# During a scan, the low parts of split weights on VectorE, scaled states and an affine map on ScalarE

## The chip, the cores and the metric

The kernel runs on one core of a Trainium2 chip. The metric is the time of one launch on the device, in microseconds (us), as the median of several runs; the kernel before has 3870.33 us (three runs, 3869.77 to 3872.68). The engines are named as in the profile: PE is TensorE's matmul and PEld its weight load, DVE is VectorE, ACT is ScalarE, POOL is GpSimd, and SP is SyncE, which issues most of the DMAs here. Each engine works off its own queue in order, and waits on semaphores for the others.

## The reference, cut to what matters

One layer of an encoder is applied to two groups of tokens: 512 prompt tokens and 1024 sample tokens, each of width 1024. It is a SwiGLU (inner width 2816), then a mixer, then a second SwiGLU, each with an RMSNorm before and after it, and with shift, scale and gate vectors that come from a conditioning vector.

```python
x = x + 0.5 * mod[:, 2] * rmsnorm(swiglu(h, f1_w1, f1_w3, f1_w2), n1_post)
z = h @ w_in                                  # 1024 -> 512 + 1952
m = concat([pool_mixer(z[..., :512]), rwkv7_mixer(token_shift(z[..., 512:]))])
x = x + mod[:, 5] * rmsnorm(m @ w_out, nm_post)
x = x + 0.5 * mod[:, 8] * rmsnorm(swiglu(h, f2_w1, f2_w3, f2_w2), n2_post)
```

The recurrent half of the mixer (8 heads of 64, two directions) is a scan over the tokens with a state S of 64x64 per head:

```python
def step(S, inp):
    r_t, w_t, k_t, v_t, na_t, b_t = inp
    sa = einsum('bhvk,bhk->bhv', S, na_t)
    S = S * w_t + sa[..., None] * b_t[:, :, None, :] + v_t[..., None] * k_t[:, :, None, :]
    return S, einsum('bhvk,bhk->bhv', S, r_t)
```

with `k_d = k * (1 + (a - 1) * kah)` for each direction. Everything is float32.

## The kernel before, in words

**Dense products.** The tokens are held in three blocks of 512 (sample 0, sample 1, prompt), features on the partitions. A float32 product is made of three fast matmuls: weights and activations are each split into a high part (`whi`, `hh`, `gh`), which is a rounded copy, and a low part (`wlo`, `hl`, `gl`), which is the value less its high part. A tile of weights, 128x512, is loaded by SP (`wraw`), rounded on ACT (`whi`), and subtracted (`wlo`, lines 498 to 505); then `mm3` issues high x high, high x low and low x high, each 128x512, which are called dense matmuls below. A tile is split three tiles before it is used.

**The scan.** It is done in chunks of 64 tokens. A macro step handles a pair of heads, in both directions and for two groups of four chunks (`gi` 0 and 1); there are 12 macro steps. Four kinds of processes carry it:

- `scan_prep` makes the decays and scaled operands of a group (`sg`, `ta`, `cs`, `AR`, `BK`, and `kd` in the tile `in_wa`: the affine map `ta * kah + kam`, line 1220, then times k), and the masked products of the chunk (`MU`).
- `scan_inv` inverts 16 triangular 64x64 matrices of a group at once. DVE transposes their diagonal 32x32 blocks from `MU` into `XN`, 62 dependent small tensor-tensor operations solve them in `XN` (on DVE for gi 0, on POOL for gi 1), DVE transposes back into `MU`, and two bursts of 16 small matmuls into a PSUM tile `sM` finish the off-diagonal blocks. The two inverses of a macro step exclude each other.
- `scan_state`, one per direction, goes through the chunks. Per chunk: matmuls for W into the bank `sb`, a copy on ACT to the upper rows of `XN` (`wsb`, line 1351), the old state times its decay (`s0p`, line 1354), matmuls with the inverse, a copy on ACT to `MU`, matmuls for the output and the new state, and the update of `SBD` on DVE from PSUM and `s0p`.
- `scan_post` normalizes the finished outputs.

While the scan runs, the first SwiGLU of the prompt tokens, the input product of the prompt tokens and the first output products fill TensorE between the scan's small matmuls.

**What sets the order.** The queue order of every engine is written out ahead by a planner in the kernel: an `Estimate` holds for each engine the time when it is free and for each tile when it is ready, from a table of costs (a subtraction of 128x512 counts 597 ns on DVE and 1226 on POOL). `run_until` steps the processes, the scan's before the dense ones where both are ready by that estimate. The engine of a low part is chosen by it: POOL, unless POOL is estimated over 4000 ns late and later than DVE (lines 502 to 504). `pick` chooses likewise between DVE and POOL for some adds of the norms and the posts. Since the helpers record every operation, nearly all instructions have line 161 in the profile; tiles tell them apart.

Of the kernel before, what the change touches and what calls it, by code (L numbers as in the profile page):

```python
# [12 lines left out]
AF = mybir.ActivationFunctionType  # L13
ALU = mybir.AluOpType
# [21 lines left out]
POOL_LATE = 4000  # L36
# [136 lines left out]
def encoder_kernel(ctx, tc, x_prompt, x_sample, c_prompt, c_sample, ada_w, ada_b, n1_pre, n1_post,  # L173
# [5 lines left out]
    V, S, G, T, SY = (Queue(est, *q) for q in (("V", nc.vector), ("S", nc.scalar), ("G", nc.gpsimd), ("T", nc.tensor),  # L179
                                               ("Y", nc.sync)))  # L180
# [33 lines left out]
    def spawn(gen, prio):  # L214
        procs.append(Proc(gen, prio))
# [36 lines left out]
                p_.ready = max(est.last + (AFTER_STATE if p_.prio == 0 else AFTER_OTHER), est.free["T"] + (0.0 if r == WAIT else r))  # L252

    flags = set()

    def until(f):
        while f() > est.free["T"] + 100:
            yield (f(),)
# [18 lines left out]
    def has(*k):  # L277
        return lambda: all(x in flags for x in k)
# [71 lines left out]
    kah = ct([P, 4], name="kah")  # L350
    kam = ct([P, 4], name="kam")
# [130 lines left out]
    class WStream:  # L482
# [12 lines left out]
        def split(self, upto):  # L495
            while self.ns <= min(upto, len(self.items) - 1):
                self.load(self.ns)
                t = self.raw.pop(self.ns)
                wh = mt([P, TB], "whi", 5, F32R)
                wl = mt([P, TB], "wlo", 5, F32R)  # L500
                S.activation(wh, t, AF.Copy)
                now = est.free["T"]
                g_, v_ = max(now, est.free["G"]) + 1200, max(now, est.free["V"]) + 600
                E = G if g_ < now + POOL_LATE or g_ < v_ else V
                E.tensor_tensor(wl, t, wh.bitcast(F32), ALU.subtract)
                self.out[self.ns] = (wh, wl)
                self.ns += 1
# [650 lines left out]
    def scan_prep(sb):  # L1158
        AR, BKt, UV, MU, Pt, PL = sb.AR, sb.BKt, sb.UV, sb.MU, sb.Pt, sb.PL
# [27 lines left out]
        for n, (m, gi) in enumerate(groups):  # L1187
            i_, hf = macros[m]
            g, p = pairs[i_]
# [14 lines left out]
            ta = st_(sb, [P, 2, GL], "ta")  # L1204
            for i, (dst, wt, o) in enumerate(((sg, w2s, 0), (ta, a2s, 8))):
# [5 lines left out]
                for d, pl in enumerate(pls):  # L1211
                    S.activation(dst[:, d, :], pl[:, 0:GL], AF.Tanh,
                                 bias=w0h[:, o + 4 * d + p:o + 4 * d + p + 1], scale=0.5)
# [3 lines left out]
            for d in range(2):  # L1217
                V.tensor_tensor_scan(rd[d](cs[:, d, :]), rst, rd[d](sg[:, d, :]), 0.0, ALU.mult, ALU.add)
            kd = ld["wa"]
            G.tensor_scalar(kd, ta, kah[:, p:p + 1], kam[:, p:p + 1], op0=ALU.mult, op1=ALU.add)  # L1220
            yield WAIT
            pinv = sg
            S.activation(flat(pinv), flat(cs), AF.Exp, scale=DECAY_C)
# [59 lines left out]
    def scan_inv(sb, gi):  # L1283
# [7 lines left out]
        eye = bass.AP(tensor=e_.tensor, offset=e_.offset, ap=[list(e_.ap[0]), [-2, 16], [1, 32]])  # L1291
        E = (V, G)[gi]
        for m in range(len(macros)):
# [37 lines left out]
    def scan_state(sb, d):  # L1331
        AR, BKt, UV, MA, MR, SBD, PL, bank = sb.AR, sb.BKt, sb.UV, sb.MA, sb.MR, sb.SBD, sb.PL, sb.bank[d]
        Wp = bank[0:64, 0:P]
        Up = bank[0:64, P:2 * P]
        for m, (i_, hf) in enumerate(macros):
            g, p = pairs[i_]
            nblk = GT[g] // GL
            nh = nblk // 2
            for c8 in range(8):
                gi, c = c8 // 4, c8 % 4  # L1340
                if c == 0:
                    yield has(("inv", m, gi))
                zero = hf == 0 and c8 == 0
                lastc = hf == nh - 1 and c8 == 7
                us = [gi * 16 + d * 8 + h * 4 + c for h in range(2)]
                if not zero:
                    mm(Wp, AR[:, gi, d, c, 0, :], SBD[:, d, :], stop=False)
                for h in range(2):
                    mm(Wp[:, h * L:(h + 1) * L], MA[64:128, us[h], :], UV[64:128, gi, d, c, h, :], start=zero)
                wsb = sb.iw[:, d * P:(d + 1) * P]  # L1350
                S.activation(wsb, Wp, AF.Copy)
                if not zero and not lastc:
                    s0p = st_(sb, [P, P], f"s0p{d}")
                    G.tensor_scalar(s0p, SBD[:, d, :], PL[:, m % 2, gi, d, c:c + 1], 0.0, op0=ALU.mult, op1=ALU.add)
                yield WAIT
                for h in range(2):
                    mm(Up[:, h * L:(h + 1) * L], MA[0:64, us[h], :], wsb[:, h * L:(h + 1) * L])
                S.activation(UV[0:64, gi, d, c].rearrange("p h f -> p (h f)"), Up, AF.Copy)
                yield WAIT
                if not lastc:  # L1360
                    for h in range(2):
                        hs_ = slice(64 * h, 64 * h + 64)
                        mm(bank[hs_, 0:L], BKt[:, gi, d, c, hs_], UV[:, gi, d, c, h, :])
                yo = 256 + c * L
                if not zero:
                    for h in range(2):
                        hs_ = slice(64 * h, 64 * h + 64)
                        mm(bank[hs_, yo:yo + L], SBD[hs_, d, hs_], AR[hs_, gi, d, c, 1, :], stop=False)
                for h in range(2):
                    mm(bank[64 * h:64 * h + 64, yo:yo + L], UV[:, gi, d, c, h, :], MR[:, us[h], :], start=zero)  # L1370
                if not lastc:
                    for h in range(2):
                        hs_ = slice(64 * h, 64 * h + 64)
                        pl_ = PL[hs_, m % 2, gi, d, c:c + 1]
                        if zero:
                            V.tensor_scalar(SBD[hs_, d, hs_], bank[hs_, 0:L], pl_, None, op0=ALU.mult)
                        else:
                            V.scalar_tensor_tensor(SBD[hs_, d, hs_], bank[hs_, 0:L], pl_, s0p[hs_, hs_],
                                                   ALU.mult, ALU.add)
                if c == 3:  # L1380
                    t = 2 * hf + gi
                    gb = t if d == 0 else nblk - 1 - t
                    if t == 0 and i_ not in sb.yT:
                        if i_ >= 1:
                            yield has(("post", i_ - 1))
                        if i_ not in sb.yT:
                            sb.yT[i_] = st_(sb, [P, GT[g]], "yT")
                    o = sb.yT[i_][:, gb * GL:(gb + 1) * GL]
                    if d == 1:
                        o = rev(o)  # L1390
                    if t >= nh:
                        V.tensor_tensor(o, o, bank[:, 256:512], ALU.add)
                    else:
                        S.activation(o, bank[:, 256:512], AF.Copy)
                    flags.add(("st", m, gi, d))
                yield WAIT
# [182 lines left out]

    with tc.tile_pool(name="late", bufs=1, reuse_waits="tile") as lp:  # L1580
        sb = ScanBufs(lp)

        spawn(scan_state(sb, 0), 0)
        spawn(scan_state(sb, 1), 0)
        spawn(scan_inv(sb, 0), PRIO_INV)
        spawn(scan_inv(sb, 1), PRIO_INV)
        spawn(scan_prep(sb), PRIO_PREP)
        spawn(scan_post(sb), PRIO_POST)

        run_until(has(("m", 1), ("m", 0)))  # L1590

    with tc.tile_pool(name="tail", bufs=1, reuse_waits="tile") as tp:

# [32 lines left out]
```

## Time and profile before

| | |
|---|---|
| median of the runs | 3870.33 us (3869.77 to 3872.68) |
| the profiled execution | 3878.62 us, its span 3876.6 us |
| mean granted TensorE clock | 0.936 of full speed |
| busy in the span: PE, DVE, ACT, POOL | 3649.0, 1977.2, 1364.7, 1704.0 us |
| the scan (first to last of its instructions) | about 1200 to 2810 us of the span |

The profile is of one execution. A row of the groups reads: line, engine, operation, written tile <- read tiles, partitions x elements, count, then the busy time in us and the mean ns of one, then the time that the engine sat idle before such instructions and what ended it. A row of the stretches has the stretch and its length, the busy us of the engines with the number of instructions, the granted clock as a share of full speed, the share of the DMA engines and GB/s. A row of the waits has who waited for whom, us in total, how often, and the longest.

### The profile page before, as it was taken

To read this page: it belongs to the slowest core of one execution; us is meant where nothing else is said; L and a number is where in the kernel's file an instruction comes from. 1 tells how busy PE (TensorE), PEld (TensorE's weight loads), DVE (VectorE), ACT (ScalarE), POOL (GpSimd) and SP (SyncE) were. 2 spreads that over 40 slices of the span, in tenths; PEclk is the share of its full clock that TensorE was granted. 3 is DMA by queue.
4 is the path that set the end of the run, shared out by engine and by line. 5 is a ranking of instruction groups with operands and counts; after the bars stand their busy time and mean duration, and the time that the engine had idled before them with its cause. 6 is when DMAs were issued, how large, how long until landed. Compare 5 with 4: busy or idle time off the path is not lost. (4 is left out here: it accounts for less than half of the span.)

```text
span 3876.6 us, 53921 instructions
## 1 busy us (share of the span) xinstructions
PE 3649.0 (94%) x19579; PEld 2752.9 (71%) x19579; DVE 1977.2 (51%) x3633; ACT 1364.7 (35%) x2592; POOL 1704.0 (44%) x2068
## 2 busy tenths in 40 slices
PE   7999999998999999999889988899999999999998
PEld 4667778876776667666667666566777778877886
DVE  3127352245247557765876676766348632232223
ACT  3324342234444333333334333333234432233222
POOL 2334444442233554355445355445544344444444
PEclk8999999999999989999879787789999999999999
DMA  7655343333443222222324233222245343334332
GB/s 270 238 177 160 98 144 93 98 108 117 128 135 112 63 77 66 74 71 88 120 67 121 84 115 109 88 74 71 64 136 163 102 130 98 95 98 138 94 98 76
DMA packets 557981, 432.11 MB, mean 111 GB/s; under 512 B 27029, under 2 KB 511572, under 8 KB 553620
## 3 DMA queue, kind: packets, MB, share of 16 engines
q1 hardware_dynamic: 524900, 379.90, 32.2%
q10 hardware_dynamic: 32816, 48.78, 4.0%
q8 instruction: 154, 2.52, 0.3%
q14 instruction: 111, 0.91, 0.1%
HBM read 367.23 MB, written 61.34 MB: 111 GB/s over the span
## 5 line engine op out<-in xcount | busy, mean ns | idle before, releaser
L161 POOL TENSOR_TENSOR wlo<-wraw,whi 128x512 fp32r<-128x512 f32 x863 | 1146.3, 1343 | 1778.1 <-ACT whi L161 1259.2
L161 DVE TENSOR_TENSOR y<-y,y 128x512 f32<-128x512 f32 x480 | 327.8, 685 | 870.5 <-PE y L161 869.3
L161 ACT ACTIVATE whi<-wraw 128x512 fp32r<-128x512 f32 x938 | 559.6, 622 | 185.5 <-PE v L161 136.9
L161 PE MATMUL u<-hh,whi 128*128 128x512 f32 x1392 | 571.0, 410 | 12.6 <-ACT hh L161 4.4
L161 PE MATMUL v<-hh,whi 128*128 128x512 f32 x1392 | 571.8, 411 | 8.3 <-ACT zraw L161 4.2
L161 PE MATMUL u<-hl,whi 128*128 128x512 f32 x1392 | 568.0, 408 | 12.1 <-DVE hl L161 10.9
L161 PE MATMUL v<-hl,whi 128*128 128x512 f32 x1392 | 568.6, 408 | 5.1 <-DVE hl L161 5.1
L161 PE MATMUL v<-hh,wlo 128*128 128x512 f32 x1392 | 571.1, 410 | 0.0
L161 PE MATMUL u<-hh,wlo 128*128 128x512 f32 x1392 | 569.8, 409 | 0.1
L161 PE MATMUL y<-gh,whi 128*128 128x512 f32 x1056 | 429.2, 406 | 12.0 <-DVE y L161 10.5
L161 PE MATMUL y<-gl,whi 128*128 128x512 f32 x1056 | 426.9, 404 | 0.0
L161 PE MATMUL y<-gh,wlo 128*128 128x512 f32 x1056 | 425.6, 403 | 0.0
L161 POOL TENSOR_TENSOR XN<-XN 64x126 f32<-64x126 f32 (+22 forms) x744 | 311.3, 418 | 66.1 <-DVE XN L161 8.1
L161 PEld LDWEIGHTS u<-hl,whi 128*128 128x128 f32 x1392 | 268.6, 193 | 83.7 <-DVE hl L161 17.9
L161 PEld LDWEIGHTS u<-hh,whi 128*128 128x128 f32 x1392 | 268.4, 193 | 82.6 <-issue 8.3
L161 PEld LDWEIGHTS v<-hh,whi 128*128 128x128 f32 x1392 | 269.8, 194 | 76.4 <-ACT hh L161 7.1
L161 PEld LDWEIGHTS v<-hl,whi 128*128 128x128 f32 x1392 | 270.1, 194 | 72.5 <-DVE hl L161 8.8
L161 PEld LDWEIGHTS u<-hh,wlo 128*128 128x128 f32 x1392 | 268.9, 193 | 69.6 <-issue 10.1
L161 PEld LDWEIGHTS v<-hh,wlo 128*128 128x128 f32 x1392 | 270.0, 194 | 67.3 <-issue 5.9
L161 ACT ACTIVATE gh<-s 128x512 fp32r<-128x512 f32 x132 | 83.3, 631 | 636.7 <-DVE s L161 636.4
L161 PEld LDWEIGHTS y<-gh,whi 128*128 128x128 f32 x1056 | 202.3, 192 | 67.1 <-DVE y L161 11.7
L161 DVE TENSOR_TENSOR XN<-XN 64x126 f32<-64x126 f32 (+22 forms) x744 | 233.2, 313 | 23.8
(252 smaller groups left out, 4456.3 us busy)
## 6 DMA issues: line engine op xcount, KB each, us to landing
wraw<-in_f_w_dram SPq DMA_DIRECT2D x792, 256.0 KB
ada<-in_ada_w_dram SPq DMA_DIRECT2D x32, 1024.0 KB
wraw<-in_w_in_dram SPq DMA_DIRECT2D x98, 256.0 KB
xk<-xs ACTq DMA_DIRECT2D x96, 256.0 KB
xs<-y ACTq DMA_DIRECT2D x48, 256.0 KB
wraw<-in_w_out_dram SPq DMA_DIRECT2D x48, 256.0 KB
in_k<-zk SPq DMA_DIRECT2D x48, 128.0 KB
in_kk<-zkk SPq DMA_DIRECT2D x48, 128.0 KB
```

Of the source, the lines that this page charges most:

```text
L161: return f(*args, **kw)
```

## The change

A flag says that the scan is running. While it does, every low part of a weight tile is made on DVE. The scaled state `s0p` is made on ACT, as a copy with a scale per partition, and the affine map of `scan_prep` on ACT, as an identity with a scale and a bias per partition. POOL keeps the inverses of gi 1, some multiplies and adds of `scan_prep` and `scan_post`, and what `pick` gives it. The planner's costs and rules are unchanged otherwise; since they see other engines busy, the written order of all engines is another one within the scan.

```diff
     flags = set()
+    scanning = []
...
                 S.activation(wh, t, AF.Copy)
                 now = est.free["T"]
                 g_, v_ = max(now, est.free["G"]) + 1200, max(now, est.free["V"]) + 600
-                E = G if g_ < now + POOL_LATE or g_ < v_ else V
+                E = G if not scanning and (g_ < now + POOL_LATE or g_ < v_) else V
                 E.tensor_tensor(wl, t, wh.bitcast(F32), ALU.subtract)
...
             kd = ld["wa"]
-            G.tensor_scalar(kd, ta, kah[:, p:p + 1], kam[:, p:p + 1], op0=ALU.mult, op1=ALU.add)
+            S.activation(kd, ta, AF.Identity, scale=kah[:, p:p + 1], bias=kam[:, p:p + 1])
...
                     s0p = st_(sb, [P, P], f"s0p{d}")
-                    G.tensor_scalar(s0p, SBD[:, d, :], PL[:, m % 2, gi, d, c:c + 1], 0.0, op0=ALU.mult, op1=ALU.add)
+                    S.activation(s0p, SBD[:, d, :], AF.Copy, scale=PL[:, m % 2, gi, d, c:c + 1])
...
         sb = ScanBufs(lp)
+        scanning.append(sb)
...
         run_until(has(("m", 1), ("m", 0)))
+        scanning.clear()
```

The order of POOL before, in the middle of the first inverse of gi 1 (XN is the inverse's work tile, s0p a scaled state, wlo a low part):

```order
L161 TENSOR_TENSOR XN_9076<-XN_9076 64x100
L161 TENSOR_TENSOR XN_9076<-XN_9076 64x4x25
L161 TENSOR_SCALAR s0p_9948<-SBD_9077,PL_9079 128x128
L161 TENSOR_SCALAR s0p_9954<-SBD_9077,PL_9079 128x128
L161 TENSOR_TENSOR wlo_9969<-wraw_9759,whi_9968 128x512
L161 TENSOR_TENSOR XN_9076<-XN_9076 64x96
L161 TENSOR_TENSOR XN_9076<-XN_9076 64x4x24
```

The same place of POOL's order with the change:

```order
L161 TENSOR_TENSOR XN_9076<-XN_9076 64x100
L161 TENSOR_TENSOR XN_9076<-XN_9076 64x4x25
L161 TENSOR_TENSOR XN_9076<-XN_9076 64x96
L161 TENSOR_TENSOR XN_9076<-XN_9076 64x4x24
L161 TENSOR_TENSOR XN_9076<-XN_9076 64x115
```

The two scaled states and the low part that stood between two pairs of the inverse's operations are gone from POOL; in this inverse nothing is left between its 62 operations, where 16 rows stood before.

The order of DVE with the change, in the second inverse of gi 0 (SBD is the update of a direction's state, y an accumulation of a dense product):

```order
L161 TENSOR_TENSOR XN_9076<-XN_9076 64x5x22
L161 TENSOR_TENSOR wlo_10656<-wraw_10432,whi_10655 128x512
L161 SCALAR_TENSOR_TENSOR SBD_9077<-sb_9080,PL_9079,s0p_10594 64x64 x2
L161 SCALAR_TENSOR_TENSOR SBD_9077<-sb_9081,PL_9079,s0p_10624 64x64 x2
L161 TENSOR_TENSOR y_9302<-y_9302,y_10661 128x512
L161 TENSOR_TENSOR XN_9076<-XN_9076 64x126
L161 TENSOR_TENSOR XN_9076<-XN_9076 64x6x21
```

Before, this inverse held no low part; now it holds nine, and 47 rows of other work in all instead of 26.

The order of ACT with the change, at the chunk that belongs to these updates (XN<-sb is the copy of W, MU<-sb the copy behind the inverse):

```order
L161 ACTIVATE XN_9076<-sb_9080 64x128
L161 ACTIVATE s0p_10594<-SBD_9077,PL_9079 128x128
L161 ACTIVATE gh_10605<-s_10426 128x512
L161 ACTIVATE whi_10609<-wraw_10349 128x512
L161 ACTIVATE XN_9076<-sb_9081 64x128
L161 ACTIVATE s0p_10624<-SBD_9077,PL_9079 128x128
L161 ACTIVATE MU_9075<-sb_9080 64x128
```

Each scaled state now stands on ACT right behind its direction's copy of W, ahead of the other direction's copies.

## The prediction

> **What bounds the kernel now.** I read the table of stretches first, with the span cut where the scan begins and ends.
>
> ```profile
> 0.00:1200.00 1200.00, 1136.15 (x5001) 860.05 (x5002) 483.38 (x727) 434.71 (x720) 454.44 (x431) 0.98 0.47 147
> 1200.00:2810.00 1610.00, 1488.50 (x10069) 1065.43 (x10069) 1080.23 (x2303) 574.00 (x1248) 776.87 (x1278) 0.87 0.28 85
> 2810.00:3876.60 1066.60, 1024.37 (x4511) 827.43 (x4511) 413.64 (x604) 356.02 (x624) 472.70 (x359) 0.99 0.37 112
> ```
>
> The columns are the stretch, its length, busy us of PE, PEld, DVE, ACT and POOL, the granted clock, and DMA. TensorE is the bound everywhere: it is busy 1488.5 of the scan's 1610 us. Two things cost time there: 121 us without a matmul, and a granted clock of 0.87 against 0.98 and 0.99 outside. TensorE's work does not change with the edit, so only these two can move. Second, what TensorE waited for in the scan (us, times, longest), and one wait of DVE:
>
> ```profile
> PE sM L161 <- DVE MU L161: 42.7, 24, 4.1
> ...
> DVE MU L161 <- POOL XN L161: 27.3, 10, 6.6
> ...
> PE sb L161 <- DVE SBD L161: 16.3, 14, 3.7
> PE sb L161 <- ACT MU L161: 15.2, 9, 5.6
> ```
>
> The largest wait stands right behind the inverses: sM reads MU, which DVE transposes out of XN when an inverse is done. Third, the timeline at the end of the first POOL inverse:
>
> ```profile
> 1307.21 0.39 PE L161 MATMUL v<-hh,whi 128*128 128x512 f32 x1
> 1307.44 0.39 PE L161 MATMUL v<-hl,whi 128*128 128x512 f32 x1
> ...
> 1309.29 1.29 POOL L161 TENSOR_TENSOR wlo<-wraw,whi 128x512 fp32r<-128x512 f32 x1
> ...
> 1310.65 1.86 POOL L161 TENSOR_TENSOR XN<-XN 64x45 f32<-64x45 f32 x6
> ...
> 1312.55 2.11 DVE L161 STREAM_TRANSPOSE MU<-XN 32x512 f32<-32x512 f32 x2 [4.21 <-POOL XN L161]
> ...
> 1315.53 1.67 PE L161 MATMUL sM<-MU 32*32 32x32 f32 x28 [3.10 <-DVE MU L161]
> ```
>
> Dense matmuls start 0.23 us apart. The inverse, interrupted by a low part (wlo), ends after TensorE has run out of dense work: DVE had waited 4.21 us for it, TensorE then waits 3.10 us. What this does to the clock is in three stretches of 10.2 us around it:
>
> ```profile
> 1304.60:1314.80 10.20, 7.83 (x36) 5.40 (x32) 4.61 (x7) 6.36 (x12) 8.84 (x20) 1.00 0.32 95
> 1314.80:1325.00 10.20, 9.47 (x77) 7.30 (x78) 4.85 (x8) 1.17 (x2) 4.50 (x5) 0.50 0.18 51
> 1325.00:1335.20 10.20, 10.20 (x72) 7.18 (x73) 8.34 (x16) 3.85 (x10) 4.89 (x6) 1.00 0.22 61
> ```
>
> After the gap TensorE runs 10.2 us at clock 0.50, so a gap of 3 us costs up to 5 us more. [...]
>
> **The change, part by part.** Counted in the order of the instructions, 191 low parts go from POOL to DVE (863 to 672 on POOL, 75 to 266 on DVE), 160 scaled states (s0p) and 24 affine maps (in_wa) go from POOL to ACT. The planner, which sees the freer POOL, also moves 23 adds and subtracts of posts and norms from DVE to POOL. So the change does what it says.
>
> *POOL's inverses.* POOL in the scan, the first POOL inverse alone (1259.4 to 1312.5), then the sums over the first five (their stretches together; all engines, then XN's instructions alone):
>
> ```profile
> L161 POOL TENSOR_TENSOR XN<-XN 64x126 f32<-64x126 f32 (+22 forms) x744 | 311.3, 418 | 66.1 <-DVE XN L161 8.1
> L161 POOL TENSOR_TENSOR wlo<-wraw,whi 128x512 fp32r<-128x512 f32 x189 | 254.7, 1352 | 472.6 <-ACT whi L161 439.0 <-issue 8.6 <-PE sM L161 5.8
> L161 POOL TENSOR_SCALAR s0p<-SBD,PL 128x128 f32<-128x128 f32 x160 | 69.1, 438 | 97.9 <-DVE SBD L161 92.7 <-PE sb L161 2.2 <-DMA wp<-gh 0.2
> ```
>
> ```profile
> L161 POOL TENSOR_TENSOR XN<-XN 64x126 f32<-64x126 f32 (+22 forms) x62 | 23.8, 385 | 5.9 <-DVE XN L161 1.1
> L161 POOL TENSOR_TENSOR wlo<-wraw,whi 128x512 fp32r<-128x512 f32 x8 | 10.7, 1347 | 8.9 <-ACT whi L161 8.6
> ```
>
> ```profile
> sum 266.60, PE 262.47 PEld 188.50 DVE 129.22 ACT 92.59 POOL 191.61; mean PE 52.49 PEld 37.70 DVE 25.84 ACT 18.52 POOL 38.32
> ...
> sum 266.60, PE 13.33 PEld 9.57 DVE 0.01 ACT 8.36 POOL 122.15; mean PE 2.67 PEld 1.91 DVE 0.00 ACT 1.67 POOL 24.43
> ```
>
> One of the five takes 266.6 / 5 = 53.3 us: 24.4 of XN, 38.3 - 24.4 = 13.9 of other work, and 15.0 of idling, of which XN's own dependences are 5.9 and a low part that stands in POOL's queue and waits for ACT's whi is 8.9. With the rest gone, 24.4 + 5.9 = 30 us are left, 23 less; since the new order keeps some rows between XN in the later inverses, I take 20. Against it the planner takes cover away: between the last sM matmul of the DVE inverse and the first of the POOL inverse TensorE has 87 dense matmuls on average instead of 130, 43 x 0.23 = 10 us. Ten us are gained net, more than the longest of these gaps (4.1), so they close. Their sum: of the 42.7 us, 27.3 is what DVE's transposes waited for POOL's XN alone; I take 30 for the twelve. With it goes the low clock: 12 x 10.2 / 2 = 61 us at most, nothing at least; I take 36, since not every gap is as long as the one shown. Term P: -66.
>
> *DVE's inverses.* In the new order the twelve chains of XN on DVE hold 99 low parts instead of 10, 7.4 more in each, and 71 other rows more, 5.9 in each. DVE in the scan, XN of one shape there and in a stretch where POOL is busy only 4.81 of 31 us, and the sums over the first five DVE chains (all, XN alone):
>
> ```profile
> L161 DVE TENSOR_TENSOR XN<-XN 64x126 f32<-64x126 f32 (+22 forms) x744 | 233.2, 313 | 23.8
> ...
> L161 DVE TENSOR_TENSOR y<-y,y 128x512 f32<-128x512 f32 x104 | 70.4, 680 | 71.1 <-PE y L161 70.3
> ...
> L161 DVE TENSOR_TENSOR wlo<-wraw,whi 128x512 fp32r<-128x512 f32 x62 | 56.7, 918 | 44.8 <-ACT whi L161 44.2 <-DMA in_wa<-za 0.3
> ```
>
> ```profile
> 2290.00:2321.00 31.00, 27.29 (x236) 20.34 (x234) 24.19 (x81) 8.20 (x20) 4.81 (x6) 0.78 0.25 77
> L161 DVE TENSOR_TENSOR XN<-XN 64x126 f32<-64x126 f32 (+17 forms) x42 | 10.9, 259 | 1.3
> ```
>
> ```profile
> sum 171.40, PE 163.57 PEld 114.83 DVE 146.77 ACT 51.21 POOL 45.01; mean PE 32.71 PEld 22.97 DVE 29.35 ACT 10.24 POOL 9.00
> ...
> sum 171.40, PE 12.11 PEld 8.49 DVE 94.05 ACT 6.34 POOL 0.00; mean PE 2.42 PEld 1.70 DVE 18.81 ACT 1.27 POOL 0.00
> ```
>
> A low part on DVE took 918 ns beside a busy POOL; the same size from PSUM, y<-y,y, took 680. POOL is now nearly idle during DVE's inverses, so I take 0.68 (up to 0.92): 7.4 x 0.68 = 5.0 us. The other rows: (146.8 - 94.1) / 121 rows = 0.44, x 5.9 = 2.6. Relief: XN took 313 ns, and 259 beside a quiet POOL, 62 x 0.054 = 3.3 less. A low part waits for whi with everything behind it on DVE (XN, SBD, the transposes, y): 44.2 / 62 = 0.71 us each so far. Its ends are 0 and 0.71; I take half, 0.36, since a part of it replaces waits that XN and SBD have anyhow (23.8 us before XN): 2.7. The planner adds cover: 103 dense matmuls become 127.5, 24 x 0.23 = 5.6. Net 5.0 + 2.6 - 3.3 + 2.7 - 5.6 = +1.4 us later, times 11 inverses with a predecessor = 15 us, and the clock in the proportion of term P (36 / 30), 18. Term D: +33. Its ends: with no wait the chains end earlier and the present 12.7 us of gaps behind them go (-13); with 0.71 they end 4.0 later, 11 x 4.0 x 2.2 = +97.
>
> *ACT.* Its rows in the scan:
>
> ```profile
> L161 ACT ACTIVATE whi<-wraw 128x512 fp32r<-128x512 f32 x251 | 152.4, 621 | 12.4 <-issue 4.5 <-POOL XN L161 4.5 <-PE v L161 2.2
> L161 ACT ACTIVATE XN<-sb 64x128 f32<-64x128 f32 x192 | 50.0, 268 | 252.9 <-PE sb L161 207.4 <-DVE XN L161 30.1 <-DVE y L161 7.2
> ...
> L161 ACT ACTIVATE sq<-sq,coef 128x512 f32<-128x512 f32 x16 | 12.9, 807 | 11.9 <-DVE sq L161 11.9
> L161 ACT ACTIVATE gl<-gh,mu 128x512 f32<-128x512 f32 x15 | 10.8, 718 | 2.1 <-DVE gl L161 1.9
> ```
>
> A scaled state is a copy of 128 columns (268) with a scale per partition (718 - 621 = 97): 0.365 us, between 0.268 and 0.46 (268 plus two such operands). 160 of them are 58 us; an affine map is as sq<-sq,coef, 807, 24 of them 19 us. ACT goes from 574 to 651 of 1610 us and hides it in its idling, 207 us of it before XN<-sb alone. What queues behind a scaled state is the other direction's copy of W, 0.365 later; without that cover it costs at most a doubling of TensorE's waits for ACT's MU, +15. On the other side DVE's SBD no longer stands behind POOL, which can save up to TensorE's 16.3 us for SBD. I take 0 for both together. The 23 moved adds take their time on POOL, which now has it, and free DVE of as many; 0 as well.
>
> The sum: the profiled execution took 3878.6 us (its span 3876.6), 8.3 above the median 3870.3. 3878.6 - 66 + 33 = 3845.6, less 8.3: **3837 us**.
>
> **The rivals.** *DVE takes POOL's place* (slower). The low parts in DVE's queue wait for ACT's whi and hold XN, SBD and the transposes behind them. For it: on POOL 99 of 189 waited, 439 us; DVE is in front of nearly every wait of TensorE. Against it: POOL had little else to do while it waited, and DVE comes later to its low parts. At 0.71 us a wait, 3878.6 - 66 + 97 - 8.3 = 3901; it decides from 0.54 us, where D reaches 66. *The transposes come late* (no change): POOL's chain ends sooner, but MU<-XN then stands behind DVE's new rows, so that only half of P is got: -33 + 33, 3870. For it: DVE is busy 67% of the scan already; against it: DVE sat idle 4.21 us there. *The relief is larger*: no wait for whi, all of the low clock behind POOL's inverses (61) and SBD's 16 us gained: 30 + 61 + 16 + 13 = 120, 3750.
>
> **How the numbers follow.** The forecast has 0.45, the larger relief 0.10, no change 0.14, slower 0.31. A difference under 0.2% (8 us) can't be told from none, so faster 0.55, same 0.14, slower 0.31. The forecast's own range is 3790 to 3862; the range of 8 in 10 runs from 3770 (most of the larger relief left out) to 3905 (the first rival with its wait of 0.71).
>
> **What would show it.** P right: the windows of POOL's inverses shrink from 53 to some 33 us, and the 3 us gaps before sM with their 0.50 clock are gone. D right: XN on DVE near 260 ns, DVE's low parts near 0.68 us with under 0.5 us of wait for whi. Wrong, if waits of TensorE for DVE (MU, SBD, wlo) grow above the present 59 us, or if the scan's clock stays at 0.87 although the gaps close.

## The result, and the profile after

The changed kernel takes **3784.43 us** (median of four runs, 3780.28 to 3787.52), the kernel before, on the same chip, 3870.05 us: a ratio of **0.9774, 95% interval 0.975 to 0.9798**, some 86 us or 2.3% less. Forecast were 3837 us, 33 less: the direction is right, the time lies inside the wide range (3770 to 3905), just under the forecast's own range (3790 to 3862), and the gain is two and a half times the one forecast. The profiled execution took 3780.28 us with a span of 3778.3, 98.3 less than the span before (3876.6); 13 of these come from which execution happened to be profiled. Where a run below had disturbed executions, the comparison leaves them out; the profile of one (states and maps on ACT in the old order) was disturbed itself, and is not read.

The table of stretches of the changed kernel, cut where its scan begins and ends (columns as before: stretch, length, busy us of PE, PEld, DVE, ACT and POOL, granted clock, DMA share, GB/s):

```profile
0.00:1200.00 1200.00, 1140.02 (x5010) 861.99 (x5012) 483.92 (x735) 437.66 (x725) 445.83 (x423) 0.98 0.46 147
1200.00:2710.00 1510.00, 1423.75 (x10050) 1010.86 (x10049) 1103.16 (x2473) 629.43 (x1427) 484.80 (x931) 0.92 0.30 90
2710.00:3778.30 1068.30, 1029.39 (x4525) 830.76 (x4523) 411.94 (x593) 357.00 (x625) 479.80 (x363) 0.99 0.38 113
```

Before and behind the scan nothing moved. The scan is 100 us shorter for as many matmuls (10050 against 10069). Of that, TensorE's idling is 121.5 - 86.3 = 35 us, and its busy time for the same work 1488.5 - 1423.8 = 65 us: the granted clock rose from 0.87 to 0.92. POOL went from 777 to 485 us, ACT from 574 to 629, and DVE, which took 191 low parts, from 1080 to only 1103.

The scan falls into two parts: five macro steps with plenty of dense matmuls, and seven in which the posts and norms of the finished tokens run too. Cut at the first transposes of the sixth step, before (PE's busy time, clock, DMA share, GB/s):

```profile
1206.80:1840.10 633.30, 600.66 (x4111) 0.92 0.26 76
1840.10:2810.00 969.90, 881.04 (x5918) 0.84 0.30 91
```

and after:

```profile
1210.90:1785.60 574.70, 559.04 (x4058) 0.98 0.28 82
1785.60:2710.00 924.40, 853.82 (x5922) 0.87 0.31 93
```

The early part loses 59 us (up to 12 of them since 53 matmuls, 0.23 us apart where dense, now lie behind the cut) and reaches the clock that the kernel has outside the scan (0.98 and 0.99); the late part loses 45 us, and its clock rises only from 0.84 to 0.87. In the trace's record of the granted clock, the early part before has 95.6 us at 0.50, in 13 stretches, and the late part 314.0 us; with the change these are 18.6 us, in 3 stretches, and 237.4. The longest of the 13 began 2.2 us behind a gap of 1.44 us, and TensorE shows as busy in all of it:

```profile
1372.80:1396.70 23.90, 23.90 (x120) 15.71 (x120) 9.15 (x16) 9.30 (x20) 8.01 (x15) 0.50 0.08 23
```

TensorE's waits in the early part, before:

```profile
PE sM L161 <- DVE MU L161: 24.0, 13, 3.9
PE sb L161 <- DVE SBD L161: 6.0, 5, 2.2
```

after:

```profile
PE sM L161 <- DVE MU L161: 5.5, 7, 2.1
PE sb L161 <- DVE SBD L161: 2.7, 2, 1.8
```

In the late part, before:

```profile
PE sM L161 <- DVE MU L161: 18.7, 11, 4.1
PE sb L161 <- ACT MU L161: 15.2, 9, 5.6
PE sb L161 <- DVE SBD L161: 10.3, 9, 3.7
```

after:

```profile
PE sM L161 <- DVE MU L161: 19.6, 14, 5.4
PE u L161 <- POOL hl L161: 7.4, 3, 3.5
PE sb L161 <- DVE SBD L161: 7.4, 9, 2.1
PE sb L161 <- ACT MU L161: 5.1, 5, 3.2
PE u L161 <- DVE hl L161: 4.0, 3, 1.8
```

So two kinds of waits went. In the early steps it is the one behind the inverses (MU), 24.0 to 5.5. In the late steps that one did not fall (18.7 to 19.6); there the chain of the states (SBD and ACT's MU) waits 12.5 us instead of 25.5.

The end of the first POOL inverse, which the prediction showed with a gap of 3.10 us, now reads in the timeline of the changed kernel:

```profile
1299.71 4.95 POOL L161 TENSOR_TENSOR XN<-XN 64x78 f32<-64x78 f32 x12
...
1308.95 2.17 DVE L161 STREAM_TRANSPOSE MU<-XN 32x512 f32<-32x512 f32 x2
...
1312.00 1.17 PE L161 MATMUL sM<-MU 32*32 32x32 f32 x32 [0.35 <-ACT s L161]
```

POOL is done at 1304.66, 4.3 us before DVE starts to transpose, and TensorE does not wait for it. The stretch of 10.2 us behind it has a clock of 1.00:

```profile
1315.00:1325.20 10.20, 10.01 (x78) 7.17 (x79) 6.54 (x6) 7.65 (x17) 1.82 (x2) 1.00 0.13 37
```

The lengths of the inverses, as the sums over the windows of all twelve (first XN to last; all engines). Before, POOL's:

```profile
sum 602.10, PE 573.98 PEld 411.65 DVE 316.59 ACT 225.09 POOL 453.30; mean PE 47.83 PEld 34.30 DVE 26.38 ACT 18.76 POOL 37.78
```

and DVE's:

```profile
sum 467.00, PE 438.46 PEld 306.14 DVE 381.58 ACT 143.51 POOL 128.43; mean PE 36.54 PEld 25.51 DVE 31.80 ACT 11.96 POOL 10.70
```

After, POOL's:

```profile
sum 412.60, PE 388.22 PEld 259.68 DVE 246.62 ACT 181.03 POOL 345.50; mean PE 32.35 PEld 21.64 DVE 20.55 ACT 15.09 POOL 28.79
```

and DVE's:

```profile
sum 537.10, PE 513.05 PEld 367.15 DVE 422.12 ACT 214.93 POOL 52.56; mean PE 42.75 PEld 30.60 DVE 35.18 ACT 17.91 POOL 4.38
```

POOL's inverses went from 50.2 to 34.4 us each, DVE's from 38.9 to 44.8. POOL's first five alone, whose windows took 266.6 us before:

```profile
sum 161.20, PE 156.64 PEld 107.80 DVE 90.72 ACT 63.95 POOL 134.73; mean PE 31.33 PEld 21.56 DVE 18.14 ACT 12.79 POOL 26.95
```

The groups behind that, in the changed kernel's scan:

```profile
L161 DVE TENSOR_TENSOR XN<-XN 64x126 f32<-64x126 f32 (+22 forms) x744 | 194.4, 261 | 23.2 <-ACT XN L161 0.5
L161 DVE TENSOR_TENSOR wlo<-wraw,whi 128x512 fp32r<-128x512 f32 x243 | 183.4, 760 | 128.4 <-ACT whi L161 127.7
...
L161 POOL TENSOR_TENSOR XN<-XN 64x126 f32<-64x126 f32 (+22 forms) x744 | 322.4, 433 | 93.6 <-DVE XN L161 18.5 <-ACT ta L161 8.0 <-ACT sg L161 7.8
...
L161 ACT ACTIVATE s0p<-SBD,PL 128x128 f32<-128x128 f32 x160 | 62.5, 391 | 0.2
```

### The profile page after: what moved, and what is told of

Same layout as the page of the kernel before. It is cut to its first block, busy times and chain, and to the rows that moved or that the text cites. A ratio compares the mean times of both kernels' runs of the same rounds, so it can differ in the third digit from the quotient of the medians.

```text
span 3778.3 us, 53665 instructions
## 1 busy us (share of the span) xinstructions
PE 3593.2 (95%) x19579; PEld 2703.6 (72%) x19579; DVE 1999.0 (53%) x3801; ACT 1424.1 (38%) x2776; POOL 1410.4 (37%) x1716
## 5 line engine op out<-in xcount | busy, mean ns | idle before, releaser
L161 POOL TENSOR_TENSOR wlo<-wraw,whi 128x512 fp32r<-128x512 f32 x672 | 892.6, 1346 | 1294.2 <-ACT whi L161 866.5
L161 PE MATMUL u<-hh,whi 128*128 128x512 f32 x1392 | 568.2, 408 | 10.2 <-ACT zraw L161 4.0
L161 PE MATMUL v<-hh,whi 128*128 128x512 f32 x1392 | 562.4, 404 | 12.8 <-ACT hh L161 7.6
L161 PE MATMUL v<-hl,whi 128*128 128x512 f32 x1392 | 561.0, 403 | 1.0 <-DVE hl L161 1.0
L161 PE MATMUL v<-hh,wlo 128*128 128x512 f32 x1392 | 560.7, 403 | 0.0
L161 POOL TENSOR_TENSOR XN<-XN 64x126 f32<-64x126 f32 (+22 forms) x744 | 322.4, 433 | 93.6 <-DVE XN L161 18.5
L161 PEld LDWEIGHTS u<-hl,whi 128*128 128x128 f32 x1392 | 266.6, 191 | 81.5 <-DVE hl L161 12.6
L161 DVE TENSOR_TENSOR wlo<-wraw,whi 128x512 fp32r<-128x512 f32 x266 | 206.4, 781 | 150.6 <-ACT whi L161 149.8
```

The lines of the kernel that those rows point to most:

```text
L161: return f(*args, **kw)
```

## The experiments

Each run was timed in three rounds against the kernel before on the same chip. Differences below are those of the ratios times 3870, so that they do not depend on the runs of the kernel before in each batch (medians 3868.6 to 3875.5); the intervals make each about 10 us uncertain.

| run | median us | ratio, 95% interval | against before |
|---|---|---|---|
| the change | 3784.43 | 0.9774, 0.975 to 0.9798 | -87 |
| low parts alone | 3819.21 | 0.9883, 0.9854 to 0.9912 | -45 |
| states and maps alone | 3825.41 | 0.9897, 0.987 to 0.9924 | -40 |
| states alone | 3843.09 | 0.9921, 0.9898 to 0.9943 | -31 |
| new engines, order as before | 3845.67 | 0.994, 0.9916 to 0.9964 | -23 |
| states and maps alone, order as before | 3857.25 | 0.9966, 0.9948 to 0.9985 | -13 |
| order of the change, old engines | 3867.87 | 0.9997, 0.9983 to 1.0011 | -1 |
| change + long POOL inverses | 3970.57 | 1.0249, 1.0223 to 1.0275 | +96 |
| change + 11 idle POOL rows per DVE inverse | 3818.45 | 0.9856, 0.9831 to 0.9882 | -56 |
| change + 22 of them | 3848.87 | 0.9946, 0.9926 to 0.9966 | -21 |
| change, low part a tile later | 3778.69 | 0.9769, 0.9735 to 0.9803 | -89 |
| change, both inverses on POOL | 3783.54 | 0.9779, 0.9761 to 0.9797 | -86 |
| change, old choices for 23 adds | 3810.72 | 0.9827, 0.98 to 0.9854 | -67 |
| before, new choices for 23 adds | 3897.15 | 1.0051, 1.0031 to 1.0071 | +20 |
| change, all such adds on DVE | 3817.32 | 0.9854, 0.9827 to 0.9881 | -57 |
| the same, low part a tile later | 3782.68 | 0.9766, 0.9733 to 0.98 | -91 |

### The two halves of the change

Against the changed kernel, the first run puts states and maps back on POOL, the second gives the low parts back to the old rule:

```diff
-            S.activation(kd, ta, AF.Identity, scale=kah[:, p:p + 1], bias=kam[:, p:p + 1])
+            G.tensor_scalar(kd, ta, kah[:, p:p + 1], kam[:, p:p + 1], op0=ALU.mult, op1=ALU.add)
...
-                    S.activation(s0p, SBD[:, d, :], AF.Copy, scale=PL[:, m % 2, gi, d, c:c + 1])
+                    G.tensor_scalar(s0p, SBD[:, d, :], PL[:, m % 2, gi, d, c:c + 1], 0.0, op0=ALU.mult, op1=ALU.add)
```

> Only the low parts move to DVE during the scan; scaled states and affine maps stay on POOL. Theory 1 (POOL's inverses were late because of what stood between their operations, and the low parts with their waits for whi were most of it): most of the 86 us, 3795 to 3815 us, POOL's inverse windows near 38 us. Rival (the state chain: scaled states leaving POOL are what helps): little gain, 3845 us or more. Rival (DVE takes POOL's place, made up by the scaled states): slower than 3870.

```diff
-                E = G if not scanning and (g_ < now + POOL_LATE or g_ < v_) else V
+                E = G if g_ < now + POOL_LATE or g_ < v_ else V
```

> Only the scaled states and the affine maps move to ACT; low parts are placed by the old rule. Theory 1: POOL's inverse windows shrink by 3 us of 50 only and the gaps behind them stay: 3850 to 3865 us. Rival (state chain): 3800 to 3830 us, with TensorE's waits for SBD and ACT's MU at half.

Measured were -45 and -40, together -85 against -87 for both: the halves add up. The first is just above its theory's range (3795 to 3815 us). The second falls into the rival's range (3800 to 3830), but TensorE's waits for SBD and ACT's MU did not halve there, as the rival had it: they went from 31.5 us to 24.8. TensorE's wait for MU in the early steps tells them apart. With states and maps alone it stays near the 24.0 of before:

```profile
PE sM L161 <- DVE MU L161: 21.5, 13, 4.3
```

and with the low parts alone it is nearly as low as with the whole change (5.5):

```profile
PE sM L161 <- DVE MU L161: 9.0, 7, 2.8
```

In the late steps it is the other way round. With the low parts alone, TensorE waits there:

```profile
PE sb L161 <- DVE SBD L161: 26.0, 19, 3.7
PE sM L161 <- DVE MU L161: 12.9, 13, 2.2
PE sb L161 <- ACT MU L161: 10.3, 6, 3.8
```

36.3 us for the chain of the states, against 12.5 with the whole change. And on POOL the scaled states wait in the queue for DVE's update (whole scan of the same run), with the inverse's XN behind them:

```profile
POOL s0p L161 <- DVE SBD L161: 141.5, 42, 14.6
```

The late steps as a whole, with the low parts alone:

```profile
1827.40:2760.00 932.60, 845.62 (x5792) 0.83 0.30 90
```

and with states and maps alone:

```profile
1799.60:2740.00 940.40, 865.62 (x6017) 0.89 0.31 95
```

So the low parts close the gaps behind the inverses of the early steps, and leave the clock of the late ones as it was (0.83 against 0.84). States and maps alone act mostly in the late steps, and there more on the clock than on the waits: it rose from 0.84 to 0.89 and the idling fell from 88.9 to 74.8 us, but the waits for SBD and ACT's MU fell only from 25.5 to 21.9. How they raise the clock is not shown. The run with the states alone splits the second half:

```diff
-            S.activation(kd, ta, AF.Identity, scale=kah[:, p:p + 1], bias=kam[:, p:p + 1])
+            G.tensor_scalar(kd, ta, kah[:, p:p + 1], kam[:, p:p + 1], op0=ALU.mult, op1=ALU.add)
```

(on top of the old rule for low parts.)

> Only the 160 scaled states go to ACT; the affine maps stay on POOL and the low parts keep their old rule. The run with states and maps together took 3825 us. Theory: the states are what helps (each stands in the chain of the states, behind what POOL has in its queue), so 3820 to 3835 here. Rival: the 24 maps (some microseconds each on POOL before) are worth the larger part; then 3850 or more here.

It took 3843 us, between the two expectations: -31 for the 160 states, -9 more for the 24 maps, the latter within the uncertainty. A map took 0.84 us on POOL before (19.3 us for 23 of them), and not some microseconds, as the rival had it.

### Engines or order

The planner writes another order once it charges other engines. The first of these runs charges POOL as before, so that the order is the old one, and issues the instructions on the new engines; the second does so for states and maps alone; the third has the order of the change, and issues states, maps and three of four of the scan's low parts on POOL (`est.op` is the planner's charge; the lines for the states are shown, those for the others are alike):

```diff
-                    S.activation(s0p, SBD[:, d, :], AF.Copy, scale=PL[:, m % 2, gi, d, c:c + 1])
+                    est.op("G", "tensor_scalar", (s0p, SBD[:, d, :], PL[:, m % 2, gi, d, c:c + 1]), {})
+                    nc.scalar.activation(s0p, SBD[:, d, :], AF.Copy, scale=PL[:, m % 2, gi, d, c:c + 1])
...
-                    S.activation(s0p, SBD[:, d, :], AF.Copy, scale=PL[:, m % 2, gi, d, c:c + 1])
+                    est.op("S", "activation", (s0p, SBD[:, d, :], AF.Copy), dict(scale=PL[:, m % 2, gi, d, c:c + 1]))
+                    nc.gpsimd.tensor_scalar(s0p, SBD[:, d, :], PL[:, m % 2, gi, d, c:c + 1], 0.0, op0=ALU.mult, op1=ALU.add)
```

> The planner reckons as before (low parts, scaled states and maps charged to POOL), so every engine's order is cut as before, but the instructions go to DVE and ACT. POOL's inverses keep their 130 dense matmuls of cover, DVE's keep 103 while they get 7 low parts more. Theory 1 with cover from the planner: POOL's gaps gone, DVE's inverses some 6 us late each, 3820 to 3860 us. Rival (cover is not short on DVE, only the engines matter): 3785 us or less.

> Scaled states and affine maps on ACT, everything else and all of the order as before (the planner still charges POOL). The same move with a new order took 44 us off. If the engine does it (SBD no longer stands behind POOL): 3830 to 3845 us. If the new order does it: 3858 to 3872 us.

> The order as the changed kernel's planner makes it, but three of four low parts of the scan, the scaled states and the maps go to POOL as before. POOL's inverses have 87 dense matmuls of cover and again some 16 rows between their operations. Theory 1: each POOL inverse ends some 10 us behind TensorE, 12 x 10 us of gaps and as much again by the clock, 3950 to 4100 us. Rival (the new order itself brings the gain, the engines little): near 3790 us.

New engines under the old order gave -23 of the -87 (states and maps alone -13 of their -40); the new order with the old engines gave nothing. With the new engines in the old order, TensorE's wait for the inverses' MU fell from 42.7 to 30.7 us, but its waits for SBD and ACT's MU stayed (33.0 us against 31.5). The third run was expected at 3950 us or more: POOL's inverses took 42.6 us there instead of 50, and TensorE's wait for MU was 52.9 us instead of some 120. So neither engines nor order carry the gain alone. That the new order uses the freed time by placing TensorE's dense work differently is the likely reading; no run shows which rows do it.

### The price of POOL's inverses, and of DVE's

22 idle subtractions of 128x256, read by nothing, stand on POOL inside each of POOL's inverses of the changed kernel; the order of everything else is the change's.

```diff
+        junk = sb.sp.tile([P, 256], F32, name=nm("junk"), tag="junk", bufs=1) if gi == 1 else None
...
                 if j % 3 == 1:
+                    if gi == 1:
+                        for q in range(2):
+                            nc.gpsimd.tensor_tensor(junk, w2s[:, 256 * q:256 * q + 256], a2s[:, 256 * q:256 * q + 256], ALU.subtract)
                     yield CHAIN
```

> The change, with 22 idle subtractions (128x256, about 0.73 us each, read by nothing) on POOL inside each of POOL's own twelve inverses, which then take about 34 + 16 = 50 us, as long as before the change, while the order of TensorE's work stays the change's, with less cover. Theory (the prediction's term P): the waits of TensorE for MU behind POOL's inverses come back, 12 x some 5 us and the low clock behind them, 3840 to 3870. Rival: POOL's inverses now have slack, and what the change gained came from DVE's side and the states: less than 20 us are lost, under 3804.

The sum over the windows of POOL's twelve inverses in this run, TensorE's largest wait, and DVE's:

```profile
sum 606.30, PE 469.70 PEld 318.22 DVE 299.68 ACT 199.23 POOL 527.80; mean PE 39.14 PEld 26.52 DVE 24.97 ACT 16.60 POOL 43.98
```

```profile
PE sM L161 <- DVE MU L161: 97.0, 24, 14.1
DVE MU L161 <- POOL XN L161: 94.8, 11, 13.1
```

and its scan:

```profile
1200.00:2890.00 1690.00, 1461.17 (x10048) 1037.23 (x10049) 1123.61 (x2473) 630.49 (x1426) 683.77 (x1194) 0.87 0.27 80
```

The inverses are as long as before (50.5 us), and the kernel is 184 us slower than the change, 96 slower than the kernel before, which had laid more dense matmuls over them (130 against 87 for each). TensorE idles 142.6 us more (1690 - 1461.2 against 1510 - 1423.8). Half of that is its wait for MU, 97.0 us against 25.1, so 6.0 for each inverse. Another 34 is its wait for the low parts of activations that POOL makes (`hl`, 41.1 against 7.4), which share POOL's queue with the longer inverses. In the early steps alone, the wait for MU goes from 5.5 us to

```profile
PE sM L161 <- DVE MU L161: 51.0, 9, 13.0
```

which is 9.1 for each of five inverses that grew by 16.5 (32.2 to 48.7): some 7 us of each were hidden by slack. TensorE's busy time for the same work rises by 37 us, as the clock falls from 0.92 to 0.87. The theory held in its direction, at more than twice its price: it had counted some 5 us of wait behind each inverse, but not what else waits for POOL.

The same rows in DVE's inverses (`gi == 0`) make POOL busy beside DVE's XN. The loop sets two at 11 places, so 22 in each inverse, 264 in all; the second run sets one.

> The changed kernel, with 20 idle subtractions of 128x256 on POOL in each of DVE's inverses, into a tile that nobody reads and that the planner does not know: POOL's own work in these windows as before the change, and no instruction of another queue moved. Theory (the relief of DVE's operations beside a quiet POOL pays for the low parts): XN on DVE goes back from 261 to 310 ns, DVE's inverses end 3 to 5 us later, 3815 to 3850 us. Rival (the relief does not reach TensorE): within 10 us of 3784.

> As the run with 264 idle POOL subtractions, with half of them: 11 instead of 22 in each of DVE's twelve inverses (132 in all, 128x256, their result is read by nothing). Theory: the time follows how much POOL works beside DVE's XN. Then XN on DVE takes between 261 ns (the change) and 372 ns (the double dose), about 315 ns, which is what it took before the change (313), and the kernel takes between 3784 and 3849 us, about 3815; the difference to the change is then the price of the contention that the change removed from DVE's inverses. Rival: DVE's inverses have slack up to some length and only the double dose used it up; then XN still takes about 315 ns, but the kernel stays within 10 us of the change's 3784.

XN on DVE and the idle rows with the full dose, and TensorE's wait for SBD:

```profile
L161 DVE TENSOR_TENSOR XN<-XN 64x126 f32<-64x126 f32 (+22 forms) x744 | 276.7, 372 | 23.2 <-ACT XN L161 0.5
L1315 POOL TENSOR_TENSOR junk<-w2s,a2s 128x256 f32<-128x256 f32 x260 | 216.0, 831 | 17.0
```

```profile
PE sb L161 <- DVE SBD L161: 29.8, 21, 4.6
```

with half of it:

```profile
L161 DVE TENSOR_TENSOR XN<-XN 64x126 f32<-64x126 f32 (+22 forms) x744 | 233.6, 314 | 23.2 <-ACT XN L161 0.5
L1315 POOL TENSOR_TENSOR junk<-w2s,a2s 128x256 f32<-128x256 f32 x130 | 110.9, 853 | 6.8
```

XN takes 261, 314 and 372 ns with none, 11 and 22 idle rows, and the kernel +32 and +67 us on the change. The half dose gives XN the 313 ns that it had before the change: the 52 ns by which XN is slower beside that much work on POOL, and which the change took from DVE's inverses, are worth some 32 us, if the idle rows act through XN alone; they ran beside DVE's other rows in these inverses too. The price follows the dose; there is no slack that only the second half uses up. Its 39.2 us more of XN time (233.6 - 194.4) cost 0.8 us each.

### The wait for whi

Each low part is made one tile later than its high part, so that DVE finds whi ready (the loads run 7 instead of 8 ahead during the scan):

```diff
                 S.activation(wh, t, AF.Copy)
-                now = est.free["T"]
-                g_, v_ = max(now, est.free["G"]) + 1200, max(now, est.free["V"]) + 600
-                E = G if not scanning and (g_ < now + POOL_LATE or g_ < v_) else V
-                E.tensor_tensor(wl, t, wh.bitcast(F32), ALU.subtract)
+                self.flush()
+                self.late = (t, wh, wl)
+                if not scanning:
+                    self.flush()
...
+        def flush(self):
+            if self.late is None:
+                return
+            t, wh, wl = self.late
+            self.late = None
...
+            E.tensor_tensor(wl, t, wh.bitcast(F32), ALU.subtract)
...
-            self.load(i + 8)
+            self.load(i + (7 if scanning else 8))
```

> The changed kernel, with each low part of the scan issued one tile later than its high part, so that it need not wait for whi; two instead of three tiles ahead of its use, loads seven tiles ahead. DVE's wait for whi (128 us in 243 low parts now) should fall under 30 us. If that wait holds up DVE's inverses as the forecast's term of 2.7 us each has it: 3745 to 3775 us. Rival (the wait falls in time that DVE had anyway): 3780 to 3800 us.

The low parts on DVE in this run:

```profile
L161 DVE TENSOR_TENSOR wlo<-wraw,whi 128x512 fp32r<-128x512 f32 x229 | 171.1, 754 | 5.4 <-ACT whi L161 4.7
```

The wait for whi fell from 127.7 us to 4.7 and the time did not change (0.9769 against 0.9774). With both inverses on POOL it did not change either:

```diff
-        E = (V, G)[gi]
+        E = G
```

> The changed kernel with both groups' inverses on POOL, 744 XN operations less on DVE. Theory (an inverse is late by what stands in its own queue): DVE's inverse windows of 45 us become POOL's of some 33, the planner cuts the cover, TensorE's waits for DVE fall: 3735 to 3775 us. Rival (POOL's slower XN, 0.43 against 0.26 us, and contention all through eat it): 3790 us or more.

It was expected at 3735 to 3775 us, and by the rival at 3790 or more; neither came. With little else on POOL, it is no matter here which of the two engines makes the inverses of gi 0.

### The planner's choices for adds

With the change the planner gives 23 more adds and subtracts of posts and norms to POOL, which the prediction priced at nothing. All of them on DVE during the scan (42 rows), without and with the late low parts:

```diff
-        return V if max(now, est.free["V"]) + 600 <= max(now, est.free["G"]) + 1200 else G
+        return V if scanning or max(now, est.free["V"]) + 600 <= max(now, est.free["G"]) + 1200 else G
```

> The change, but while scanning the planner's choice between DVE and POOL for the adds of posts and norms always takes DVE. Theory: what is left of TensorE's idling sits in the late steps of the scan, where a post's add on POOL takes 1.65 us and more and ACT and TensorE wait for it; on DVE it takes 0.68, so 3765 to 3780. Rival: these adds stand in front of XN, SBD and the transposes on DVE, and the time is the change's or more, 3785 to 3800.

> The run before it, with each low part issued one tile later than its high part (the loads run 7 instead of 8 ahead in the scan), so that DVE does not wait for ACT's whi. Theory: the adds on DVE make DVE the tighter engine, so its 128 us of waits for whi now count for something: 3755 to 3775, below the run before it by 5 to 15. Rival: these waits fall into idling that DVE has anyhow, as in the run with this edit alone (3779 against 3784): within 5 us of the run before it.

The theory fell: DVE takes 0.69 us for an add that takes POOL 1.54, and still the kernel loses 31 us. The late low parts bring that back (-34): on a DVE with less room the wait for whi does count, or the order that goes with this edit suits it better; the two weren't separated. The next two runs fix the choices, in order, to those made for the other kernel: the change with the 23 rows back on DVE, and the kernel before with these 23 rows alone on POOL (a letter per choice and site; `...` stands for the strings).

```diff
-    def pick():
+    PICKS = dict(a=..., s=..., y=..., x=...)
+    took = dict.fromkeys("asyx", 0)
+
+    def pick(k):
+        took[k] += 1
+        return V if PICKS[k][took[k] - 1] == "V" else G
```

> The change, but the planner's choices between DVE and POOL for adds and subtracts of posts and norms are fixed, in order, to those that it made for the kernel before: 23 of them go back to DVE. Theory: DVE's time is dear in the late steps of the scan, as when all 42 went to DVE (3817 against 3784), so in proportion 23/42 x 33 = 18 us are lost: 3795 to 3810. Then these 23 rows, priced at nothing in the prediction, were part of the gain. Rival: only the rows that were on POOL before already matter, and the time stays at 3780 to 3788.

> The kernel before, with the planner's choices between DVE and POOL for adds and subtracts of posts and norms fixed to those that it made for the change: 23 rows go to POOL, nothing else is moved. Theory: they help only where POOL has been freed; on the full POOL of before they stand in front of XN, low parts and scaled states, and the time is 3870 to 3890. Rival: they help by themselves, through DVE's time alone: 3850 to 3860.

The 23 rows are worth 21 us in the changed kernel, and cost 20 in the kernel before, where POOL is full. The parts of the scan of the first run, as above:

```profile
1213.30:1786.80 573.50, 557.97 (x4074) 0.99 0.28 82
1786.80:2742.00 955.20, 869.70 (x5903) 0.84 0.30 90
```

Its early steps are as long as the change's (573.5 against 574.7); all of the loss is in the late ones (955.2 against 924.4). There TensorE now waits for the low parts of activations on DVE (4.0 with the change, and 7.4 for those on POOL):

```profile
PE u L161 <- DVE hl L161: 16.8, 9, 3.6
```

## Why the prediction was right and wrong

**What bounds it: right.** Only idling and the clock could move, and did: 35 and 65 us in the scan.

**Term P, POOL's inverses: right in the early steps, not in the late ones.** Forecast was that the early inverses go from 53 us to 33; they take 161.2 / 5 = 32.2. The gaps behind them closed where the prediction had taken its rows. By the forecast, 10 us of net gain less gaps of 4.1 left 6 to spare; the run with long inverses found some 7 in the early steps. The clock was put at 36 us for twelve gaps of some 3 us; that the run with long inverses also lost 37 us of busy time is chance, since TensorE idled 142.6 us more there. But the wait for MU only closed in the early steps (24.0 to 5.5); in the late ones it went from 18.7 to 19.6, so instead of the 30 us of gaps that I took for all twelve of POOL's inverses, 17.6 went, with DVE's inverses included. The late inverses on POOL shrank by 12.0 us, from 47.9 to 35.9; an estimate from this and the 10 us of cover that the planner takes away leaves 2 us of net gain there, less than the longest gap of 4.1.

**Term D, DVE's inverses: the parts right, the sum not borne out.** Forecast were 7.0 us longer windows before cover (5.0 + 2.6 - 3.3 + 2.7); measured are 5.8, (537.1 - 467.0) / 12, and the cover of 5.6 takes that up: +0.2 instead of +1.4 each. XN fell to 261 ns (forecast 259), a low part took 760 (680). What fell is the wait for whi: it is longer than I took (127.7 / 243 = 0.53 us against 0.36), and taking it away gains nothing measurable. Also the price of 2.2 us for each us later was too high: the run with the half dose paid 0.8. By 0.2 x 12 x 0.8, D would be some 2 us, not 33; this is an estimate.

P and D were not run without each other. Their sum is near the run with the low parts alone: -45 (interval -57 to -34) against -33, and that run has 15 of the 23 adds on POOL already.

**ACT and the adds at nothing: wrong, and the step that failed.** "I take 0 for both together" was measured at -42 (the change against low parts alone) and "0 as well" at -21, in part the same us. ACT's cost was right: a scaled state took 391 ns (forecast 365), a map 807, hidden in ACT's idling. What I set against each other were a doubling of the waits for ACT's MU, +15, and a gain of up to SBD's 16.3 us. The first had the wrong sign: that wait fell from 15.2 to 5.1. The second I bounded by the wait that the trace of before shows, which holds for the order and the clock of before. With the order kept, it held within the uncertainty: -13 (interval -20 to -6). With the order written anew, states and maps alone took off 40 us although the gaps behind the early inverses stayed (21.5 us of 24.0), and the clock of the late steps rose from 0.84 to 0.89. So the step failed where it priced the move by waits alone: the new order, and the clock that rose with it, brought more than the whole of the wait. On top of the low parts the same move also shortened the waits of the late steps, from 36.3 us to 12.5.

**The clock** makes up most of what was missed: -65 us in the scan where P and D together had -18. I counted it behind the inverses alone. But in the early steps the clock rose from 0.92 to 0.98, as high as outside the scan, and it rose in the late steps from 0.84 to 0.87, where the waits behind the inverses did not fall. Nor did only gaps as long as the prediction's (3.10 us) stand ahead of the low clock: in the early steps before, twelve of the 13 stretches at 0.50 begin within 6 us of the start of a gap of 1.2 to 3.9 us, and six of these gaps are under 2 us. In the row of 23.9 us at 0.50 TensorE was busy throughout; what kept the clock low there is not shown. The cost was also no fixed ratio to the idling, 1.2 as I had it: 37 us to 143 with long inverses, 65 to 35 for the change.

**The rivals.** *DVE takes POOL's place* was to decide from 0.54 us of wait for a low part; 0.53 were measured, and the kernel is 86 us faster, so that point was wrong. *The transposes come late*: they do, 4.3 us after POOL is done in the first inverse, but TensorE is not kept by it. *The relief is larger* (3750) named two sources that did move, SBD and the clock, and overshot by 34 us; its first condition, no wait for whi, did not come (0.53 us each).

**What would have shown it** came in the main: windows near 33, the gap of 3 us and its 0.50 gone, XN near 260, the waits of TensorE for DVE's MU and SBD down from 59 to 35, the scan's clock up from 0.87. Not so DVE's low parts: 0.76 us and 0.53 of wait, where 0.68 and under 0.5 had been named.

**Still open** is how the re-planned order does its share. It carries most of the gain (new engines alone give -23), it isn't worth anything by itself, and only 21 us of it could be given a name, the adds. Open too is what holds the clock at 0.50 in the late steps, for 237 us even with the change. A version that beats the change clearly was not found: the low parts a tile later are within its interval.

## What to carry to other kernels

Price a moved instruction by the chain it stands in, and not only by the idle time of the engine that takes it: 160 copies of 0.39 us on an idle ACT went with 31 us less, in an order written anew. Where a planner writes the order, moving work and re-planning act together, and the two runs that separate them (new engines in the old order, old engines in the new one) are cheap and tell what an estimate from the old trace cannot. And a wait that the old trace shows bounds the gain from it only in the old order and at the old clock: here 16.3 us of wait bounded the 13 us that came with the order kept, and not the 40 that came with the new one.

## What the runs showed of the hardware

In the two runs with idle rows in DVE's inverses, POOL's work beside DVE's went with a longer XN on DVE, by a nearly steady share: 110.9 us of subtractions on POOL added 39.2 us to XN on DVE, 216.0 us added 82.3, so 0.35 and 0.38 us for each. On POOL an idle row took 853 ns in the mean with half the dose, 831 with the full dose (there 734 in the median, 2861 at most), and 793 inside POOL's own inverses.

The clock's price was not in proportion to the idle time: with long inverses TensorE idled 142.6 us more and was busy 37 us longer for the same work, while the change, which took away 35 us of idling in the scan, gained 65 us of busy time.
